# Block inverses of an RWKV-7 recurrence: alternating the two heads of a pair in the small matmuls that build them

## The chip, the cores and the metric

One core of a Trainium2 chip (trn2). The metric is device time in microseconds of one execution of the whole program, lower is better. TensorE is called PE below, its weight loads PEld, VectorE DVE, ScalarE ACT, GpSimd POOL; SP issues the DMAs.

## The reference, cut to what matters

The model is two layers on 512 tokens of 1024 features. Layer 0 mixes tokens by RWKV-7, layer 1 by a Conformer convolution; each is followed by cross-attention to 256 memory tokens and a conv-gated MLP. Only the recurrence of layer 0 is touched by the change:

```python
def rwkv7_step(S, inp):
    r_t, dec_t, k_t, v_t, kk_t, a_t = inp
    sa = jnp.einsum('bhij,bhj->bhi', S, -kk_t)
    S = (S * dec_t[:, :, None, :]
         + sa[..., None] * (kk_t * a_t)[:, :, None, :]
         + v_t[..., None] * k_t[:, :, None, :])
    y = jnp.einsum('bhij,bhj->bhi', S, r_t)
    return S, y
```

There are 16 heads of 64. The kernel does not step through 512 tokens. It cuts them into 8 chunks of 64; inside a chunk the terms `sa` depend on one another through a strictly lower triangular 64x64 matrix, so that each (head, chunk) needs the inverse of one unit triangular 64x64 matrix. That is 128 inverses. Each is built from two 32x32 inverses on the diagonal and a 32x32 block that couples them.

## The kernel before, in words

All weight products (`gemm_cols`, `mm3`, lines 179 to 223) split both operands into a high and a low fp32r part and make three matmuls of 128x128 weights on 512 columns (L181, L182, L183). The weights come by DMA, ACT rounds them to the high part (L176) and DVE subtracts (L177). Layer 0 runs the products for k, r and v one after another, eight output blocks each. After each block a callback does the pair's own work (`k_done`, `r_done`, `v_done`) and then `step(n)`, which at fixed places starts a stage of the inverses. A pair is two heads, head h on partitions 64h to 64h+63.

The 16 heads are two groups of four pairs. For each group there are two stages:

- `subst_a` (lines 563 to 602), after the blocks k 3 (group 0) and r 4 (group 1). **Set-up products**: for each of four pairs one PSUM tile ("kv", one bank); for head h, chunk c and half u one matmul of 64x32 weights (`bk`) on 64 or 32 columns (`AR`), L577. The output stands on partitions 64h+32u. DVE masks the diagonal blocks (L580), two ACT copies take the off-diagonal ones into `TT` (L584). Then DVE alone inverts all 32x32 diagonal blocks at once by forward substitution, 30 steps of a multiply (L598) and an add (L600), with 32x32 transposes before (L586).
- `subst_b` (lines 604 to 635), after the blocks r 1 (group 0) and v 5 (group 1). DVE transposes the inverses into `D1` (L608) and `DT` (L610). **Coupling products**: for head h and half of the 32 (pair, chunk) blocks, 16 matmuls of 32x32 weights on 32 columns into one kv bank (L622), one ACT copy of 32x512 into `RT` (L624); then, for head h and half again, 16 such matmuls (L632) and one ACT copy into `TT` (L634). With q1 = partitions 64h to 64h+31 and q2 = the next 32, L622 reads q1 and writes q2, L632 reads q2 and writes q1. `TT` also gets two ACT copies of `DT` per head (L616, L617) and a memset on POOL (L615).

The kv tag has two buffers (line 139), which also serve the products of keys and values of the memory (L912, L936). They stand between the others as fillers. Each engine works through a queue in order. That order is fixed when the kernel is built: the framework's scheduler takes the instructions in the order of the program, as priorities, moves ready ones ahead by its own estimates of their durations, and adds the semaphores.

After v comes `chain` (lines 637 to 759), the recurrence over the eight chunks, which multiplies by `TT` in L711; there the two heads of a pair already alternate in the innermost loop and write one bank.

A plain-fp32 matmul of the program stands in the trace as two matmul instructions, each with its own weight load: 256 matmuls of L577 are 512 rows, 128 of L622 and of L632 are 256 each.

Of the kernel before, what the change touches and what calls it, by code (L numbers as in the profile page):

```python
# [21 lines left out]
NCH = T // C  # L22
# [88 lines left out]
class Builder:  # L111
# [451 lines left out]
    def subst_a(self, grp):  # L563

        nc = self.nc
        TT = self.TT[grp]
        rho = self.rho[:, grp * 32 : grp * 32 + 32]
        c4 = lambda: self.t(self.r1, [128, 32, 32], "c4", bufs=4)
        A = c4()
        for pl in range(4):  # L570
            p = grp * 4 + pl
            ps = self.ps("kv").rearrange("p (c t) -> p c t", t=64)
            for h in range(2):
                rows = slice(64 * h, 64 * h + 64)
                for c in range(NCH):
                    for u in range(2):
                        nc.tensor.matmul(ps[64 * h + 32 * u : 64 * h + 32 * u + 32, c, 0 : 64 - 32 * u],  # L577
                                         self.bk[p][rows, c, h, 32 * u : 32 * u + 32],
                                         self.AR[rows, 0, p, c * C + 32 * u : (c + 1) * C], start=True, stop=True)
            nc.vector.tensor_tensor(out=A[:, pl * 8 : pl * 8 + 8, :], in0=ps[:, :, 0:32],  # L580
                                    in1=self.c("m32").unsqueeze(1).to_broadcast([128, 8, 32]), op=ALU.mult)
            for h in range(2):
                q1 = slice(64 * h, 64 * h + 32)
                nc.scalar.copy(TT[q1, pl * 8 : pl * 8 + 8, 32:64], ps[q1, :, 32:64])  # L584
        N = c4()
        nc.vector.transpose(out=N, in_=A.rearrange("p g t -> p t g"))  # L586
        rt = self.t(self.r1, [128, 32], "rt", bufs=1)
        nc.vector.transpose(out=rt, in_=rho)
        nc.vector.tensor_tensor(out=N, in0=N, in1=rt.unsqueeze(2).to_broadcast([128, 32, 32]), op=ALU.mult)
        Ti = c4()  # L590
        nc.scalar.copy(Ti, N)
        nc.vector.memset(Ti.rearrange("p t s -> p (t s)")[:, 0 : 32 * 32 : 33], 1.0)
        prs = c4().rearrange("p g t -> p (g t)")
        for s in range(1, 31):
            n = 31 - s
            pr = prs[:, s % 2 * 512 :]
            pv = pr[:, : n * s].rearrange("p (t j) -> p t j", j=s)
            nc.vector.tensor_tensor(out=pv, in0=N[:, s + 1 :, s : s + 1].to_broadcast([128, n, s]),  # L598
                                    in1=Ti[:, s : s + 1, 0:s].to_broadcast([128, n, s]), op=ALU.mult)
            nc.vector.tensor_tensor(out=Ti[:, s + 1 :, 0:s], in0=Ti[:, s + 1 :, 0:s], in1=pv, op=ALU.add)  # L600
        nc.vector.tensor_tensor(out=Ti, in0=Ti, in1=rt.unsqueeze(1).to_broadcast([128, 32, 32]), op=ALU.mult)
        self.sub = TT, Ti, c4

    def subst_b(self, grp):
        nc = self.nc
        TT, Ti, c4 = self.sub
        D1 = c4()
        nc.vector.transpose(out=D1.rearrange("p g j -> p j g"), in_=Ti.rearrange("p t j -> p j t"))  # L608
        DT = c4()
        nc.vector.transpose(out=DT.rearrange("p g t -> p t g"), in_=Ti)  # L610
        RT = c4().rearrange("p g t -> p (g t)")
        for h in range(2):
            q1 = slice(64 * h, 64 * h + 32)
            q2 = slice(64 * h + 32, 64 * h + 64)
            nc.gpsimd.memset(TT[q2, :, 0:32], 0.0)  # L615
            nc.scalar.copy(TT[q1, :, 0:32], DT[q1])  # L616
            nc.scalar.copy(TT[q2, :, 32:64], DT[q2])  # L617
            for half in range(2):
                ps = self.ps("kv")
                for j in range(16):  # L620
                    g = half * 16 + j
                    nc.tensor.matmul(ps[q2, j * 32 : (j + 1) * 32], TT[q1, g, 32:64], D1[q1, g, :],  # L622
                                     start=True, stop=True)
                nc.scalar.copy(RT[q2, half * 512 : half * 512 + 512], ps[q2, :])  # L624
        for h in range(2):
            q1 = slice(64 * h, 64 * h + 32)
            q2 = slice(64 * h + 32, 64 * h + 64)
            for half in range(2):
                ps = self.ps("kv")
                for j in range(16):  # L630
                    g = half * 16 + j
                    nc.tensor.matmul(ps[q1, j * 32 : (j + 1) * 32], RT[q2, g * 32 : (g + 1) * 32],  # L632
                                     DT[q2, g, :], start=True, stop=True)
                nc.scalar.copy(TT[q1, half * 16 : half * 16 + 16, 32:64],  # L634
                               ps[q1, :].rearrange("p (g t) -> p g t", t=32))

    def chain(self):

# [741 lines left out]
```

## Time and profile before

| what | value |
|---|---|
| median of 3 runs (lowest to highest) | 1705.75 us (1701.08 to 1711.86) |
| the profiled execution's own time | 1704.39 us |
| its span | 1702.6 us |
| PE busy | 1668.6 us (98%) |
| DVE busy, ACT busy | 1096.9 us (64%), 782.5 us (46%) |
| mean granted clock of TensorE | 0.99 |

The span runs from the first to the last instruction of the program; 1.8 us of the execution lie outside it. Busy PE is not PE at its peak: the rows of matmuls overlap. The stages of the inverses lie between 101 and 299 us of the span; `chain` follows from 309 us.

### The profile page before, as it was taken

The page shows a single profiled execution, that of the slowest core. Times are in us where ns is not written, and L with a number is a line of the kernel's source. Part 1 is how long each engine was busy: PE and PEld are TensorE (multiplying, and loading weights), DVE is VectorE, ACT ScalarE, POOL GpSimd, SP SyncE. Part 2 cuts the span into 40 slices and gives each one's busy share as a digit, 9 for nine tenths or more (in the row PEclk, how much of TensorE's full clock was granted, in tenths as well). Part 3 has the DMA queues.
Part 4 walks back from the last instruction along what each step waited for, and adds up shares of the span by engine and source line. Part 5 has one row for each costly group of instructions (what it writes and reads, how often), then busy time and mean ns, then how long its engine had stood idle before and what let it go on. Part 6 is the DMA issues. An engine that isn't in the chain of part 4 may idle for free. (4 is left out here: it accounts for less than half of the span.)

```text
span 1702.6 us, 23980 instructions
## 1 busy us (share of the span) xinstructions
PE 1668.6 (98%) x9662; PEld 1328.1 (78%) x9662; DVE 1096.9 (64%) x1777; ACT 782.5 (46%) x1216; POOL 73.2 (4%) x101
## 2 busy tenths in 40 slices
PE   7999989999999999999999999999999999999998
PEld 6585668888788888888888877767888888888887
DVE  4679975344676567777753358996666677777333
ACT  5865634445435335444432256665444444444222
POOL 0000000000000000000000014340000000000000
PEclk9999999999999999999999999999999999999999
DMA  6323312001533232333333332223412233333332
GB/s 230 122 85 108 107 56 75 27 14 33 158 120 113 63 124 88 100 99 97 92 98 92 105 118 62 62 88 99 137 63 74 89 99 100 98 91 93 101 91 84
DMA packets 55151, 159.77 MB, mean 94 GB/s; under 512 B 6144, under 2 KB 10368, under 8 KB 55040
## 3 DMA queue, kind: packets, MB, share of 16 engines
q1 hardware_dynamic: 55040, 158.24, 29.9%
q8 instruction: 76, 1.25, 0.3%
q14 instruction: 35, 0.29, 0.1%
HBM read 150.55 MB, written 7.67 MB: 93 GB/s over the span
## 5 line engine op out<-in xcount | busy, mean ns | idle before, releaser
L176 ACT CAST wh<-raw 128x1024 fp32r<-128x1024 f32 (+1 forms) x225 | 233.2, 1037 | 496.6 <-PE g L182 406.6
L182 PE MATMUL g<-xl,wh 128*128 128x512 f32 x1152 | 452.2, 393 | 4.2 <-DVE xl L177 3.6
L181 PE MATMUL g<-xh,wh 128*128 128x512 f32 x1152 | 454.0, 395 | 0.6 <-ACT xh L176 0.6
L183 PE MATMUL g<-xh,wl 128*128 128x512 f32 x1152 | 451.9, 392 | 1.6 <-DVE wl L177 1.6
L177 DVE TENSOR_TENSOR wl<-raw,wh 128x1024 fp32r<-128x1024 f32 (+1 forms) x225 | 272.2, 1210 | 159.0 <-ACT wh L176 158.5
L182 PEld LDWEIGHTS g<-xl,wh 128*128 128x128 f32 x1152 | 217.5, 189 | 54.0 <-DVE xl L177 6.6
L183 PEld LDWEIGHTS g<-xh,wl 128*128 128x128 f32 x1152 | 217.5, 189 | 49.3 <-DVE wl L177 2.3
L181 PEld LDWEIGHTS g<-xh,wh 128*128 128x128 f32 x1152 | 217.4, 189 | 48.8 <-ACT xh L176 1.7
L181 PE MATMUL g<-ah,wh 128*128 128x512 f32 (+1 forms) x374 | 140.9, 377 | 0.0
L182 PE MATMUL g<-al,wh 128*128 128x512 f32 (+1 forms) x374 | 140.8, 377 | 0.0
L183 PE MATMUL g<-ah,wl 128*128 128x512 f32 (+1 forms) x374 | 140.8, 377 | 0.0
L1050 DVE TENSOR_TENSOR z<-g,rs 128x512 f32<-128x512 f32 x88 | 60.4, 688 | 71.3 <-PE g L183 69.7
L182 PEld LDWEIGHTS g<-al,wh 128*128 128x128 f32 x374 | 70.4, 188 | 13.0
L183 PEld LDWEIGHTS g<-ah,wl 128*128 128x128 f32 x374 | 70.4, 188 | 12.9
L181 PEld LDWEIGHTS g<-ah,wh 128*128 128x128 f32 x374 | 70.4, 188 | 12.7
L1170 POOL TENSOR_TENSOR dg<-i,wsp 128x256 fp32r<-128x256 f32 x70 | 48.3, 723 | 668.2 <-DVE wsp L1124 584.1
L1192 DVE SCALAR_TENSOR_TENSOR h<-u,cdw,h 128x512 f32<-128x512 f32 x98 | 73.8, 753 | 2.4
L176 ACT CAST ah<-tmp 128x512 fp32r<-128x512 f32 x44 | 27.3, 621 | 100.9 <-DVE z L1049 95.8
L321 DVE TENSOR_TENSOR x<-x,g 128x512 f32<-128x512 f32 x39 | 26.8, 688 | 67.5 <-PE g L183 67.5
L1055 DVE SCALAR_TENSOR_TENSOR tmp<-z,fdw,tmp 128x512 f32<-128x512 f32 x88 | 66.0, 752 | 2.9
L1054 DVE SCALAR_TENSOR_TENSOR tmp<-z,fdw,tmp 128x512 f32<-128x512 f32 x88 | 65.5, 746 | 0.4 <-ACT tmp L1053 0.4
L1053 ACT ACTIVATE tmp<-z,fdw 128x512 f32<-128x512 f32 x88 | 63.3, 722 | 4.8 <-DVE z L1050 1.5
(331 smaller groups left out, 2458.3 us busy)
## 6 DMA issues: line engine op xcount, KB each, us to landing
raw<-wi SPq DMA_DIRECT2D x84, 512.0 KB, 3.5
raw<-wo SPq DMA_DIRECT2D x33, 512.0 KB, 3.5
raw<-wv SPq DMA_DIRECT2D x16, 512.0 KB, 3.6
raw<-cwi SPq DMA_DIRECT2D x14, 512.0 KB, 3.5
raw<-wq SPq DMA_DIRECT2D x12, 512.0 KB, 4.6
raw<-wxo SPq DMA_DIRECT2D x12, 512.0 KB, 3.6
raw<-wo SPq DMA_DIRECT2D x16, 384.0 KB, 3.1
raw<-wk SPq DMA_DIRECT2D x10, 512.0 KB, 3.5
```

The source lines that it names most:

```text
L176: self.nc.scalar.copy(h, src)
L177: self.nc.vector.tensor_tensor(out=l, in0=src, in1=h, op=ALU.subtract)
L181: mm(out, lh, rh, start=start, stop=False)
L182: mm(out, lh, rl, start=False, stop=False)
L183: mm(out, ll, rh, start=False, stop=stop)
L321: self.nc.vector.tensor_tensor(out=self.x[:, n, :], in0=self.x[:, n, :], in1=ps, op=ALU.add)
L1050: nc.vector.tensor_tensor(out=z[:, 2:], in0=ps, in1=rs(), op=ALU.mult)
L1053: nc.scalar.activation(y, z[:, 2:], AF.Copy, scale=cw(2))
L1054: nc.vector.scalar_tensor_tensor(out=y, in0=z[:, 1 : T + 1], scalar=cw(1), in1=y, op0=ALU.mult, op1=ALU.add)
L1055: nc.vector.scalar_tensor_tensor(out=y, in0=z[:, 0:T], scalar=cw(0), in1=y, op0=ALU.mult, op1=ALU.add)
L1170: nc.gpsimd.tensor_tensor(out=dg[:, h], in0=i2.unsqueeze(1).unsqueeze(1).to_broadcast([128, 2, 2, 64]), in1=wsp[:, :, i, h, 2 * g : 2 * g ...
L1192: nc.vector.scalar_tensor_tensor(out=ac, in0=u[:, jt : jt + T], scalar=cw(jt), in1=ac if n else ln["c"], op0=ALU.mult, op1=ALU.add if n el ...
```

## The change

In `subst_a` the loops over chunk and half go outside and the loop over the two heads innermost: the same matmuls, in another order. In `subst_b` the same is done in both coupling products, and the tile is taken per half rather than per head and half: one kv bank holds the results of both heads (on disjoint partitions), 32 matmuls rather than 16, and two ACT copies empty it. So a group takes four kv tiles in `subst_b` and not eight. The memset and the copies of `DT` of both heads come ahead of the products in program order. The number, shape and engine of all instructions stay.

```diff
-            for h in range(2):
-                rows = slice(64 * h, 64 * h + 64)
-                for c in range(NCH):
-                    for u in range(2):
+            for c in range(NCH):
+                for u in range(2):
+                    for h in range(2):
+                        rows = slice(64 * h, 64 * h + 64)
                         nc.tensor.matmul(ps[64 * h + 32 * u : 64 * h + 32 * u + 32, c, 0 : 64 - 32 * u],
...
+        q1 = [slice(64 * h, 64 * h + 32) for h in range(2)]
+        q2 = [slice(64 * h + 32, 64 * h + 64) for h in range(2)]
         for h in range(2):
-            q1 = slice(64 * h, 64 * h + 32)
-            q2 = slice(64 * h + 32, 64 * h + 64)
-            nc.gpsimd.memset(TT[q2, :, 0:32], 0.0)
-            nc.scalar.copy(TT[q1, :, 0:32], DT[q1])
-            nc.scalar.copy(TT[q2, :, 32:64], DT[q2])
-            for half in range(2):
-                ps = self.ps("kv")
-                for j in range(16):
-                    g = half * 16 + j
-                    nc.tensor.matmul(ps[q2, j * 32 : (j + 1) * 32], TT[q1, g, 32:64], D1[q1, g, :],
+            nc.gpsimd.memset(TT[q2[h], :, 0:32], 0.0)
+            nc.scalar.copy(TT[q1[h], :, 0:32], DT[q1[h]])
+            nc.scalar.copy(TT[q2[h], :, 32:64], DT[q2[h]])
+        for half in range(2):
+            ps = self.ps("kv")
+            for j in range(16):
+                g = half * 16 + j
+                for h in range(2):
+                    nc.tensor.matmul(ps[q2[h], j * 32 : (j + 1) * 32], TT[q1[h], g, 32:64], D1[q1[h], g, :],
                                      start=True, stop=True)
-                nc.scalar.copy(RT[q2, half * 512 : half * 512 + 512], ps[q2, :])
...
+            for h in range(2):
+                nc.scalar.copy(RT[q2[h], half * 512 : half * 512 + 512], ps[q2[h], :])
...
+                for h in range(2):
+                    nc.tensor.matmul(ps[q1[h], j * 32 : (j + 1) * 32], RT[q2[h], g * 32 : (g + 1) * 32],
+                                     DT[q2[h], g, :], start=True, stop=True)
+            for h in range(2):
+                nc.scalar.copy(TT[q1[h], half * 16 : half * 16 + 16, 32:64],
+                               ps[q1[h], :].rearrange("p (g t) -> p g t", t=32))
```

The removed loops of L632 and L634, left out here, are those of L622 and L624 with q1 and q2 exchanged.

## Rows read from the trace of the kernel before

**Rows 1.** Windows of 10 us: each engine's busy us and instructions, PEclk, DMA share, GB/s.

```profile
100.00:110.00 10.00, 10.00 (x158) 8.35 (x157) 8.08 (x18) 5.81 (x12) 0.32 (x1) 1.00 0.30 93
110.00:120.00 10.00, 9.86 (x102) 7.61 (x101) 7.66 (x18) 7.57 (x14) 0.00 (x0) 1.00 0.29 93
...
180.00:190.00 10.00, 9.44 (x42) 6.93 (x41) 9.77 (x24) 5.00 (x10) 1.32 (x2) 1.00 0.22 61
190.00:200.00 10.00, 8.31 (x108) 6.81 (x108) 9.85 (x15) 9.01 (x12) 0.57 (x1) 0.66 0.66 228
200.00:210.00 10.00, 10.00 (x166) 6.76 (x166) 6.72 (x11) 4.09 (x7) 0.00 (x0) 1.00 0.01 2
...
220.00:230.00 10.00, 9.99 (x197) 8.00 (x195) 6.34 (x8) 3.49 (x9) 0.00 (x0) 1.00 0.18 56
...
290.00:300.00 10.00, 10.00 (x154) 8.55 (x151) 0.00 (x0) 2.88 (x5) 0.00 (x0) 0.61 0.02 3
```

**Rows 2.** Waits from 95 to 310 us: total us, times, longest us.

```profile
PE g L182 <- DVE xl L177: 3.6, 3, 2.6
...
DVE c L580 <- PE kv L577: 4.1, 5, 1.2
```

**Rows 3.** Groups of instructions by line, 101 to 310 us: weight loads.

```profile
L577 PEld LDWEIGHTS kv<-AR,BK 64*32 64x32 f32 x512 | 12.7, 106 | 3.0 <-issue 2.6 <-ACT tt L584 0.3
...
L632 PEld LDWEIGHTS kv<-c,c 32*32 32x32 f32 x256 | 10.1, 123 | 2.5 <-issue 1.8 <-ACT tt L634 0.7
...
L622 PEld LDWEIGHTS kv<-c,tt 32*32 32x32 f32 x256 | 8.4, 108 | 2.6 <-DVE c L608 1.1 <-issue 0.6 <-ACT tt L617 0.6
```

**Rows 4.** Timeline, weight loads: start us, length us, line, shape, count.

```profile
101.74 1.62 PEld L577 LDWEIGHTS kv<-AR,BK 64*32 64x32 f32 x64 [0.36 <-issue]
...
190.11 3.01 PEld L622 LDWEIGHTS kv<-c,tt 32*32 32x32 f32 x96 [1.11 <-DVE c L608]
...
200.16 1.08 PEld L622 LDWEIGHTS kv<-c,tt 32*32 32x32 f32 x32 [0.59 <-ACT tt L617]
...
204.48 3.01 PEld L632 LDWEIGHTS kv<-c,c 32*32 32x32 f32 x96 [0.36 <-issue]
...
284.09 2.10 PEld L622 LDWEIGHTS kv<-c,tt 32*32 32x32 f32 x64 [0.35 <-PE g L182]
...
290.91 4.15 PEld L632 LDWEIGHTS kv<-c,c 32*32 32x32 f32 x96 [0.25 <-issue]
...
296.28 1.78 PEld L632 LDWEIGHTS kv<-c,c 32*32 32x32 f32 x32 [0.65 <-ACT tt L634]
...
317.14 0.55 PEld L711 LDWEIGHTS h<-tmp,tt 64*64 64x64 f32 x16
```

**Rows 5.** Windows of 0.2 us, L577 alone: PE and PEld busy and count, PEclk.

```profile
102.00:102.20 0.20, 0.20 (x15) 0.20 (x10) 1.00 1.08 410
102.40:102.60 0.20, 0.20 (x22) 0.20 (x18) 1.00 0.73 266
```

**Rows 6.** Timeline around `subst_b` of group 0: DVE, PE and ACT.

```profile
193.53 1.22 DVE L177 TENSOR_TENSOR wl<-raw,wh 128x1024 fp32r<-128x1024 f32 x1
...
194.81 0.80 PE L183 MATMUL g<-xh,wl 128*128 128x512 f32 x1 [1.57 <-DVE wl L177]
...
196.71 0.58 ACT L624 COPY c<-kv 32x512 f32<-32x512 f32 x1
...
201.39 0.58 ACT L624 COPY c<-kv 32x512 f32<-32x512 f32 x1 [0.64 <-PE kv L622]
```

**Rows 7.** Timeline, large matmuls after `subst_b` of group 1.

```profile
299.14 0.63 PE L181 MATMUL g<-xh,wh 128*128 128x512 f32 x1
299.57 0.63 PE L182 MATMUL g<-xl,wh 128*128 128x512 f32 x1
...
305.01 0.39 PE L182 MATMUL g<-xl,wh 128*128 128x512 f32 x1
305.24 0.39 PE L183 MATMUL g<-xh,wl 128*128 128x512 f32 x1
```

More of the change, by code (lines that the diff above doesn't have):

```diff
@@ L625, in subst_b @@
[L625 to L635, printed above, removed]
+            nc.gpsimd.memset(TT[q2[h], :, 0:32], 0.0)
@@ new lines, in subst_b @@
+        for half in range(2):
+            ps = self.ps("kv")
+            for j in range(16):
+                g = half * 16 + j
+                for h in range(2):
[4 more added lines that the diff above has]
+                               ps[q1[h], :].rearrange("p (g t) -> p g t", t=32))
```

## The prediction, made before the changed kernel was run

> **What bounds the kernel now.** I read four views in turn: windows of 10 us over the stretch where the inverses are built (who is full there), the waits of that stretch (who waits for whom), the groups by line (how many instructions the change touches), and the timeline close to each stage (their spacing). The windows show two regimes. At 100 to 120, 200 to 210, 220 to 230 and 290 to 300 us PE is full (9.86 to 10.00 of 10) and DVE has room; at 180 to 200 us DVE is full (9.77, 9.85) and PE is not [rows 1]. The waits agree: DVE waits 4.1 us for the set-up products, and PE waits 3.6 us for DVE's low halves [rows 2]. So a microsecond saved on PE is worth a microsecond in the first regime, as long as the work behind it moves up too, and nothing while DVE is full.
>
> The touched matmuls are 1024 instructions, 512 in L577 and 256 each in L622 and L632 [rows 3]. They are small, and what they cost is their spacing, not the length of a row (a load lasts 0.106 us, and many are under way at once). With the last load's length taken off [rows 4]:
> - L577: (1.62 - 0.11) / 63 = 24.0 ns from one to the next;
> - L622 and L632: (3.01 - 0.11) / 95 = 30.5 ns;
> - L711, where the heads alternate: (0.55 - 0.135) / 15 = 27.7 ns, with 64 weight columns and 64 moving columns (0.135 for its last load is an estimate; at 0.11 it would be 29.3).
>
> So the alternating L711 streams twice the columns of L622 in less time for each instruction. I read that as two heads under way at once: one tile of 64 columns would need about twice the 30.5 ns. L577 gives a second sign. Its two halves u already stand on different output columns, while the two heads follow each other; at the change from head 0 to head 1, half of the way through the block, 18 loads touch a window of 0.2 us where 10 touch one in the middle of a head [rows 5]. There the end of one head runs beside the start of the next.
>
> **The change part by part.** No instruction is added or taken away; the alternation is what can save.
>
> 1. L577, eight blocks of 64 rows. If both heads run side by side, a block falls from 64 x 24.0 ns = 1.54 us to 0.77. Bounds: 0 (the spacing is already under that of L711) and 0.77 us a block. I take the latter, the half, since where the heads meet the density nearly doubles [rows 5]. Group 0: 4 x 0.77 = 3.1 us. PE is full there, and DVE has 1.92 + 2.34 = 4.3 us of idle time at 100 to 120 us [rows 1], more than 3.1, so the substitution, which then fills DVE up to 200 us, can start earlier by as much. Group 1: 3.1 us, PE full (9.99), DVE at 6.34. Sum 6.2, bounds 0 and 6.2.
> 2. L622 of group 0, 128 rows. The first 96, 3.01 us from 190.11, stand in a wait for DVE: PE's next large matmul starts at 194.81 whatever they take, since DVE gets to its weights at 193.53 [rows 6]. Worth nothing. The last 32 (1.08 us from 200.16 [rows 4]) are on PE's path: half is 0.5 us; if they fit into that wait as well, 1.1. I take 0.5; at the other end 0.
> 3. L632 of group 0, 128 rows: 3.01 us for 96 and in proportion 1.0 for the rest, 4.0 us with PE full at 200 to 210 us. Halved: 2.0. Bounds 0 and 2.0.
> 4. L622 of group 1, 128 rows: 2.10 us for 64 [rows 4], so 4.2, with PE busy throughout. Halved: 2.1. Bounds 0 and 2.1.
> 5. L632 of group 1, 128 rows: 4.15 + 1.78 = 5.9 us [rows 4], since the granted clock fell on the way (0.61 over 290 to 300 us [rows 1]); at full clock they would take the 4.0 of group 0. Halved at the same clock: 3.0. Bounds 0 and, at full clock throughout, 5.9 - 2.0 = 3.9.
> 6. The large matmuls after it. At the low level of the clock (1.2 GHz) they start 0.43 us apart, at the high one (2.4 GHz) 0.23 [rows 7]. The clock fell after PE had done little but small matmuls, and came back, with large ones under way, between 300 and 305 us. From the end of the 96 at 295.1, less the 1.78 us of the last 32, that is 3.1 to 8.1 us of large ones, 7 to 19 of them, which cost 0.20 us each more than at full clock: 1.4 to 3.8 us, in the middle 2.6. A stretch of small ones half as long may or may not spare this. Bounds 0 and 3.8; I take 0, the row as it stands.
> 7. Waits. A product now waits for two ACT copies of 0.58 us, one for each head, before its bank and its half of `RT` are free, where it waited for one [rows 6]. PE has large matmuls to put between, as before. Behind such a wait stand the next weight products, and behind them DVE and ACT. I charge one copy, 0.6 us; bounds 0 and four copies, 2.3.
>
> Sum: 6.2 + 0.5 + 2.0 + 2.1 + 3.0 - 0.6 = 13.2 us. The profiled execution took 1704.4 (a span of 1702.6 and 1.8 around it), so 1691.2. It lies 1.4 us under the median of 1705.75; for a median of the changed kernel I say 1692. Past 309 us nothing is touched, and I assume that the recurrence and the layers behind it move up unchanged. 1% is 17 us, about what a measurement of this kernel can tell from no change; the forecast lies just inside it.
>
> **A rule that speaks against it.** The two heads of L711 read different row halves, write one bank, and still start 27.7 ns apart [rows 4]. The Trainium skill (TensorEngine Tiling (Array Packing), "Restrictions and Gotchas") says that different row tiles cannot access the same PSUM bank at once. By that rule items 1 to 5 would give nothing, by the row they give the sum above. The trace doesn't bear the rule out for heads that also write different partitions of the bank, as they do here.
>
> **Rivals.**
> - *The bank makes the heads take turns.* At 32x32, each alternated pair then takes its two spacings of 30.5 ns, L577 its 24.0, and only the charge for waits is left: 1704.4 + 0.6 = 1705.0. For it: no row before has two 32x32 tiles side by side. Against it: L711, and the dense window of L577, whose heads share a bank too. This is what the Trainium skill's rule above would make of it.
> - *A floor for each instruction.* L622 and L632 fall from 30.5 to L577's 24.0 and L577 stays. For it: 24.0 and 27.7 are close although the columns differ. Against it: the dense window of [rows 5]. Gain: on the three stages of items 3 to 5, 128 x 6.5 ns = 0.8 us each, 2.4, less 0.6: 1702.6. The Trainium skill (TensorE: Matmul & The Clock Gate, "Wait — 56ns, not 53.3ns?") states such a floor, about 25 ns from start to start; the mean of 24.0 lies a little under it.
> - *DVE keeps it.* DVE is full before 200 us and the order of its queue is fixed. If earlier set-up products don't let the substitution start earlier, because DVE's other work stands before it, items 1 and 2 are lost: 13.2 - 6.7 = 6.5 us, 1697.9. For it: 9.77 and 9.85 of 10. Against it: DVE's 4.3 idle us before, and its waits for just these products [rows 2].
> - *The clock holds.* With half the time in small matmuls the clock doesn't fall at group 1: items 5 and 6 give 3.9 + 2.6, which is 3.5 more than taken: 1687.7. For it: the price stands there, 5.9 us and the large ones behind. Against it: the small ones that are left still come in one run.
> - *PE stands behind ACT (slower).* In group 0 the copies L624 were late, at 196.71 and 201.39 us, as ACT was at 9.01 of 10 and works in order. If PE's fixed order puts a product that needs both heads' copies ahead of the weight products, PE stands still from about 192 to 202, 10 us, and then has 16 large matmuls at the low clock (3.2 us); in group 1 it waits for four copies (2.3). That is 15.5 against 13.2 + 0.6: 1706.1. It decides from about 14 us of standing still.
>
> **How the numbers follow.** Chances: forecast 0.42, clock holds 0.20, DVE keeps it 0.20, floor 0.07, bank 0.04, PE behind ACT 0.07. The forecast's own range is 1688 to 1695 (item 6 in part; item 7 at its end). The whole range, 1684 to 1704, reaches from the clock rival with item 6 at its end, all of item 2 and no charge for waits (1685.3), less the 1 us or so by which runs differ, to beyond the floor rival; it leaves out the bank and ACT rivals and what may lie outside all of these. Faster by over 1% (under 1688.7): two thirds of the clock rival and a seventh of the forecast, 0.19. Slower by over 1% (over 1722.8): only if PE stands far longer, 0.02. Within 1%: 0.79.
>
> **What would show it.** Right would be: L577 in blocks of 64 of about 0.9 us and not 1.62; L622 and L632 15 to 16 ns apart, 64 rows in about 1.1 us; the first substitution step earlier by 2 to 3 us and `chain` by 12 to 14; PE still waiting for DVE near 190 us. Wrong would be: spacings near 24 or 30 ns (floor, bank); halved spacings but a `chain` that starts no more than 7 us earlier (DVE); PE waiting for L624 or L634 (ACT); or a difference made after `chain` has begun, where I see none.

## The result, and the profile after

| | before | after |
|---|---|---|
| median of 4 runs each (lowest to highest) | 1707.88 us (1701.08 to 1711.86) | 1688.01 us (1686.79 to 1693.23) |
| the profiled execution's own time | 1704.39 us | 1689.21 us |
| its span | 1702.6 us | 1687.3 us |
| its mean granted clock | 0.990 | 0.992 |

The ratio of the medians is 0.9884, 95% interval 0.9853 to 0.9915. The kernel became 1.2% faster: inside the range given, 4 us under the forecast of 1692, and just past the 1% that the forecast had stopped short of (the interval reaches to 0.85%; the repeat, e10, lies past 1% with all of its interval). It is the time of the rival "the clock holds" (1687.7).

In the changed kernel the first coupling product is L623 (was L622), its copy L626, the last copy L635 and the first product of `chain` L663; L577 and L632 keep their numbers. The timeline of the weight loads gives the new spacing, to be set against [rows 4]:

```profile
100.51 0.92 PEld L577 LDWEIGHTS kv<-AR,BK 64*32 64x32 f32 x64 [0.35 <-issue]
...
188.03 2.10 PEld L623 LDWEIGHTS kv<-c,tt 32*32 32x32 f32 x128 [1.13 <-DVE c L608]
...
200.69 2.10 PEld L632 LDWEIGHTS kv<-c,c 32*32 32x32 f32 x128 [0.36 <-issue]
...
278.45 2.10 PEld L623 LDWEIGHTS kv<-c,tt 32*32 32x32 f32 x128 [0.35 <-PE g L182]
...
281.96 2.10 PEld L632 LDWEIGHTS kv<-c,c 32*32 32x32 f32 x128 [0.37 <-issue]
```

All four coupling products take 2.10 us for 128 rows, (2.10 - 0.11) / 127 = 15.7 ns from one to the next, where it was 30.5. L577 takes (0.92 - 0.11) / 63 = 12.9 ns, where it was 24.0. The groups by line, 100 to 295 us, say the same in sums. Beside [rows 3] the busy time fell and the count did not; a load lasts as long as before, but for L632 (123 to 108 ns), part of which had run at the low clock:

```profile
L577 PEld LDWEIGHTS kv<-AR,BK 64*32 64x32 f32 x512 | 7.6, 106 | 4.2 <-issue 3.3 <-ACT tt L584 0.9
L632 PEld LDWEIGHTS kv<-c,c 32*32 32x32 f32 x256 | 4.2, 108 | 0.7 <-issue 0.7
L623 PEld LDWEIGHTS kv<-c,tt 32*32 32x32 f32 x256 | 4.2, 108 | 1.5 <-DVE c L608 1.1 <-PE g L182 0.4
```

The windows of 10 us (columns as in [rows 1]):

```profile
100.00:110.00 10.00, 9.51 (x159) 7.05 (x157) 7.02 (x17) 6.35 (x11) 0.32 (x1) 1.00 0.33 104
...
180.00:190.00 10.00, 9.30 (x153) 7.01 (x153) 9.77 (x20) 4.17 (x7) 1.89 (x2) 1.00 0.33 85
190.00:200.00 10.00, 7.53 (x36) 5.05 (x30) 9.76 (x16) 9.07 (x12) 0.00 (x0) 0.66 0.52 172
...
240.00:250.00 10.00, 7.14 (x20) 4.23 (x19) 9.88 (x21) 3.82 (x7) 0.00 (x0) 0.74 0.17 59
...
280.00:290.00 10.00, 10.00 (x202) 8.42 (x196) 0.64 (x1) 5.08 (x9) 0.00 (x0) 1.00 0.32 101
290.00:300.00 10.00, 9.88 (x105) 8.31 (x103) 2.58 (x4) 3.47 (x8) 0.00 (x0) 1.00 0.25 92
```

Three things are to be seen. PE is still idle for 2.5 us of 190 to 200 while DVE is full, as said. At 240 to 250 us PE waits for DVE too (7.14), and the clock fell there (0.74). In the trace of before PE is idle in the same way at 250 to 260 us, and the clock stayed at 1.00:

```profile
250.00:260.00 10.00, 6.51 (x25) 4.42 (x26) 9.94 (x21) 5.73 (x9) 0.00 (x0) 1.00 0.22 64
```

And at group 1 the granted clock now stays at 1.00 through both products and what follows, where it had fallen to 0.61. The large matmuls behind L632 show it, 0.24 us apart and not 0.43 [rows 7]:

```profile
284.44 0.40 PE L181 MATMUL g<-xh,wh 128*128 128x512 f32 x1
284.68 0.40 PE L182 MATMUL g<-xl,wh 128*128 128x512 f32 x1
```

**Where the time came from.** Landmarks of the two traces, us from the span's start:

| landmark | before | after | earlier by |
|---|---|---|---|
| first set-up block | 101.74 | 100.51 | 1.2 |
| first substitution step, group 0 | 138.88 | 136.78 | 2.1 |
| first set-up block of group 1 | 217.96 | 212.03 | 5.9 |
| first substitution step, group 1 | 230.54 | 224.07 | 6.5 |
| transposes into `D1`, group 1 | 272.95 | 267.30 | 5.7 |
| first product of `chain` | 308.96 | 294.07 | 14.9 |
| last output of `chain` | 435.84 | 419.48 | 16.4 |
| end | 1702.62 | 1687.35 | 15.3 |

The largest step, 9.2 us, lies between the transposes of group 1 and `chain`. The 1.2 us at the top came before anything that the change touches: the traced run of before had 3.4 us at the low clock from 29.4 us on, that of after none there.

**A line through all the runs.** Every run comes with its mean granted clock c. The low level is half of full speed, so the time that a run spent there is about 2 (1 - c) of its time. Later jobs brought 42 runs of before, with a median of 1711.5 us, from 1699.96 us (c = 0.992) to 1715.13 us (0.983). A straight line through them has a slope of 0.41 us for each microsecond at the low level and meets zero such time at 1690.1 us. With the same slope for all kernels the residual is 0.9 us (117 runs). I call that intercept the time at full clock; for each kernel it is the mean over its runs. By the scatter of those runs it is uncertain by 0.1 us (before) to 0.9 us (e5). It splits each difference below into "work", the difference at full clock, and clock. The split rests on the line; no run was held at one clock level.

### The profile page after: what moved, and what is told of

The parts are those of the page before. It is cut to its first block, busy times and chain, and to the rows that moved or that the text cites. A ratio compares the mean times of both kernels' runs of the same rounds, so it can differ in the third digit from the quotient of the medians.

```text
span 1687.3 us, 23987 instructions
## 1 busy us (share of the span) xinstructions
PE 1650.6 (98%) x9662; PEld 1312.3 (78%) x9662; DVE 1096.3 (65%) x1777; ACT 782.2 (46%) x1216; POOL 73.1 (4%) x101
## 5 line engine op out<-in xcount | busy, mean ns | idle before, releaser
L182 PEld LDWEIGHTS g<-al,wh 128*128 128x128 f32 x374 | 70.4, 188 | 12.9
L183 PEld LDWEIGHTS g<-ah,wl 128*128 128x128 f32 x374 | 70.4, 188 | 12.9
```

The costliest lines, as they stand in the source:

```text
L182: mm(out, lh, rl, start=False, stop=False)
L183: mm(out, ll, rh, start=False, stop=stop)
```

## The experiments

Each job ran the kernel before on the same chip. "Low" is the median time at the low level.

| kernel | median us (runs) | ratio to before, 95% | low us | at full clock |
|---|---|---|---|---|
| before | 1711.5 (42) | | 51.3 | 1690.1 |
| after, first comparison | 1688.0 (4) | 0.9884 (0.9853 to 0.9915) | 25.3 | 1677.9 |
| after, again (e10) | 1687.5 (4) | 0.9865 (0.9839 to 0.9891) | 21.9 | 1678.9 |
| e1 set-up only | 1704.0 (11) | 0.9962 (0.9946 to 0.9979) | 44.3 | 1686.2 |
| e2 coupling only | 1686.8 (5) | 0.9870 (0.9841 to 0.9898) | 13.5 | 1680.6 |
| e3 one bank, heads in turn | 1697.5 (10) | 0.9931 (0.9910 to 0.9951) | 25.5 | 1686.4 |
| e4 alternating, two banks | 1700.5 (11) | 0.9942 (0.9923 to 0.9961) | 34.0 | 1686.1 |
| e5 group 1 only | 1694.5 (4) | 0.9903 (0.9875 to 0.9932) | 25.4 | 1684.0 |
| e6 group 0 only | 1697.6 (5) | 0.9928 (0.9904 to 0.9952) | 27.2 | 1686.1 |
| e7 group 1 twice | 1700.7 (5) | 0.9936 (0.9915 to 0.9957) | 37.4 | 1684.3 |
| e8 wait filled | 1686.1 (4) | 0.9856 (0.9837 to 0.9875) | 18.5 | 1678.7 |
| e9 one copy | 1688.1 (4) | 0.9862 (0.9843 to 0.9880) | 23.6 | 1678.0 |
| e11 e8 and e9 | 1688.6 (4) | 0.9861 (0.9840 to 0.9883) | 20.3 | 1680.1 |
| e12 e8, set-up as before | 1689.3 (4) | 0.9866 (0.9847 to 0.9885) | 18.6 | 1681.6 |

**The two parts apart.** e1 is the kernel before with the first part of the change's diff alone, the new loop order of L577; e2 has the other part alone, the new `subst_b`.

> Only the set-up products (L577) alternate; the coupling products stay as before. My theory: a block of 64 falls from 1.62 us to 0.92, but little of it arrives, since the block's neighbours (the ACT copies that free its bank, the r and k callbacks that PE waits for) set the pace: 1 to 2 us faster, spacing of the coupling products still 31 ns, and the clock falls at group 1 as before. Rival 'every PE microsecond counts': 8 x 0.7 = 5.6 us faster. Rival 'clock': the shift alone moves where the clock falls, which gives anything within 4 us either way.

The blocks of L577 fall to 0.92 us. Eight of them save 5.6 us. But e1's trace, which leads that of before by 1.4 us at the first block (100.39 against 101.74), leads by 3.6 at the first product of `chain` (305.38 against 308.96): 2.2 arrive, 0.8 gained up to the first substitution step of group 0 and 1.2 over the set-up of group 1. The waits of e1 while group 1 is set up, 217 to 229 us, show who takes the rest:

```profile
DVE c L580 <- PE kv L577: 1.6, 2, 1.1
...
PEld h L553 <- DVE tmp L550: 0.9, 1, 0.9
...
PEld kv L577 <- ACT tt L584: 0.6, 1, 0.6
```

In the trace of before DVE waits there for L577 for 2.9 us, PE for L550 for 0.2 and for L584 not at all. So PE got ahead of the work between the blocks and then stood. At full clock the part is worth 3.9 us. In the median it is 7.1 us (the 26 runs of before on that chip had 1711.06), since e1 also spent less time at the low level: outside all three expectations.

> Only the coupling products alternate, both heads in one bank; the set-up products stay as before. My theory: the coupling products carry the gain, by halved spacing (16 ns) and by the clock that no longer falls at group 1: 12 to 15 us faster, the recurrence starts at about 296 us and not 309. Rival 'halved rows alone': the products give 2 + 2 + 3 us and the clock still falls: 7 to 8 us faster, the recurrence starts at about 301 us.

e2 carries the gain: both halves of each product in one run of 128 rows of 2.10 us, `chain` from 295.15 us, 24 us less in the median, where 12 to 15 were expected. In work that is 9.5 us, above the 7.6 of items 2 to 5; the rest is clock (51.3 to 13.5 us low). In work e1 and e2 together make 13.4 us, the whole change 11.6 (both comparisons of it). In the median e2 alone is as fast as the whole change (1686.8 against 1688.0 and 1687.5): on top of e2 the set-up's alternation shows no gain there, only in the time at full clock.

**Pairing, or the shared bank?** e3 keeps the one bank for two heads but runs the heads one after the other; e4 alternates them but gives each its bank. Both have the set-up of before.

```diff
-            for j in range(16):
-                g = half * 16 + j
-                for h in range(2):
+            for h in range(2):
+                for j in range(16):
+                    g = half * 16 + j
```

The second product is edited in the same way.

> As the run with the coupling products alone, one bank for both heads, half the tiles and the same order of the copies, but inside a bank all 16 of head 0 come ahead of head 1. My theory: no pairing, so 31 ns from one to the next, the small matmuls of group 1 last 8 us and the clock falls there: within 3 us of the kernel before. Rival 'fewer banks to wait for': the gain is in the arrangement, 8 us or more faster although the spacing stays at 31 ns.

```profile
188.02 4.20 PEld L623 LDWEIGHTS kv<-c,tt 32*32 32x32 f32 x128 [1.12 <-DVE c L608]
...
289.47 6.34 PEld L632 LDWEIGHTS kv<-c,c 32*32 32x32 f32 x128 [0.65 <-issue]
```

In this timeline of e3 the spacing is that of before, (4.20 - 0.11) / 127 = 32 ns, and at group 1 the clock falls again, so that the same 128 rows take 6.34 us. Its windows there:

```profile
280.00:290.00 10.00, 10.00 (x158) 8.17 (x157) 2.45 (x2) 5.79 (x9) 0.00 (x0) 0.84 0.37 112
290.00:300.00 10.00, 10.00 (x132) 9.07 (x131) 0.00 (x0) 2.30 (x4) 0.00 (x0) 0.50 0.01 3
```

So the halved spacing does need the alternation. `chain` starts only 1.0 us earlier than before, in a trace that led by 2.1 us at the first set-up block. But the median fell by 13.6 us: far outside the 3 us expected, and by the number it is the rival's 8 us or more. By the line 3.7 us of that is work, the rest less time at the low level, which one trace does not place. The whole first product of group 0 now stands in one row ahead of the wait for DVE; that this and the fewer banks to empty make the 3.7 us is not shown.

```diff
-            ps = self.ps("kv")
+            pss = [self.ps("kv") for _ in range(2)]
...
-                    nc.tensor.matmul(ps[q2[h], j * 32 : (j + 1) * 32], TT[q1[h], g, 32:64], D1[q1[h], g, :],
+                    nc.tensor.matmul(pss[h][q2[h], j * 32 : (j + 1) * 32], TT[q1[h], g, 32:64], D1[q1[h], g, :],
```

The copies read `pss[h]`, and the second product is edited in the same way.

> As the run with the coupling products alone, alternating, but each head writes a bank of its own, so a half takes both kv banks. My theory: the heads run side by side in one bank as well as in two, so the spacing is 16 ns in both, and the next half waits for two banks to be emptied, with 0.6 to 1.2 us of copies four times: 0 to 4 us slower than one bank. Rival 'the bank holds the heads up': with two banks the spacing falls well under 16 ns and the time is shorter than with one bank.

The timeline of e4's weight loads at group 1:

```profile
285.75 1.09 PEld L623 LDWEIGHTS kv<-c,tt 32*32 32x32 f32 x64 [0.35 <-PE g L182]
...
288.47 1.08 PEld L623 LDWEIGHTS kv<-c,tt 32*32 32x32 f32 x32 [0.36 <-ACT c L626]
289.59 0.19 PEld L181 LDWEIGHTS g<-xh,wh 128*128 128x128 f32 x1
290.01 1.08 PEld L623 LDWEIGHTS kv<-c,tt 32*32 32x32 f32 x32 [0.24 <-issue]
```

With a bank for each head 64 alternating rows take 1.09 us, 15.6 ns: as in one bank. So sharing the bank costs no spacing. What two banks cost is order: the second half of this product waits for a copy, its heads fall apart, and each stands alone at 31 ns. e4 is 5.5 us slower than e2 at full clock and spent 20 us more at the low level. Pairing and sharing belong together here: one of them alone (e3, e4) gives 4 us of work, both give 9.5.

**Which group, and what of it is the clock?** e5 uses the new `subst_b` for group 1 only, e6 for group 0 only, with the set-up of before; the old one is kept as `subst_b_seq`, and `subst_b_alt` is that of the change. e5's line is shown; e6 has `grp == 0`.

```diff
+        (self.subst_b_alt if grp == 1 else self.subst_b_seq)(grp)
```

> The coupling products alternate in group 1 alone; group 0 and the set-up products stay as before. My theory (rows and clock): the 128 rows of each product of group 1 fall from 4.2 and 5.9 us to 2.1 and 2.1, the clock stays at its high level there, and from the end of the substitution to the start of the recurrence 8 to 9.5 us are gained; in the median 9 to 15 us, since runs in which the clock falls for longer than in the profiled one gain more. Rival 'rows alone': the clock still falls at group 1 and 5 us are gained there, 5 to 7 in the median.

From the transposes of group 1 to `chain` e5 takes 26.88 us, before 36.01, after 26.77: 9.1 us as expected, and its clock is 1.00 from 280 to 300 us. In the median it gained 15.6 us, just over the 9 to 15 expected. The windows of e5 show that the clock fell at group 0 instead, over 200 to 220 us, where the second product is still done head by head (1.00 over 200 to 210 us in after, but also in before, which has the same order there):

```profile
200.00:210.00 10.00, 10.00 (x130) 5.98 (x129) 6.18 (x10) 2.78 (x5) 0.00 (x0) 0.76 0.02 3
210.00:220.00 10.00, 10.00 (x39) 5.61 (x39) 1.62 (x3) 0.58 (x1) 0.00 (x0) 0.73 0.16 53
```

> The coupling products alternate in group 0 alone; group 1 and the set-up products stay as before. My theory: the first product stands under PE's wait for DVE and gains nothing, its last 32 rows and the second product give about 3 us, and the clock falls at group 1 as before: 2 to 5 us faster in the median. With the run on group 1 alone the two gains add up to that of both groups (about 1.3%). Rival 'the low clock of group 0 is half the story': 8 us or more, with several us less at the low level around 190 to 210 us.

Expected were 2 to 5 us, measured 12.5: missed, and by the number it is the rival, 8 us or more. In work the part is worth 4.0 us; the rest is time at the low level (51.3 to 27.2). One trace each doesn't place it: over 190 to 200 us e6 has 0.83 where before has 0.66, 3.4 us less at the low level. e6's trace has the clock at 1.00 over 200 to 210 us, and falls at group 1, like before:

```profile
280.00:290.00 10.00, 10.00 (x205) 8.79 (x203) 1.11 (x1) 3.98 (x8) 0.00 (x0) 0.87 0.30 100
290.00:300.00 10.00, 10.00 (x56) 7.78 (x56) 0.00 (x0) 1.56 (x3) 0.00 (x0) 0.62 0.08 20
```

The two groups don't add up: 15.6 and 12.5 us alone, 24 together in e2. In work they do as far as can be told, 6.1 + 4.0 = 10.1 against 9.5. A lesson in reading: what is not additive here is the clock, not the work.

e7 asks whether the clock holds because the small matmuls are denser or because they are over sooner. It runs each alternating product of group 1 twice (the second time over the same results), so the density was to be that of after and the length that of before. Both products have this edit.

```diff
-            for j in range(16):
+            for j in list(range(16)) * (1 + grp):
```

> As the changed kernel, but in group 1 each coupling matmul is issued twice (the same result is written again), so the small products last as long as they did before the change, 4.2 us each, while the two heads still run side by side. Theory 'density': it is the pairing that holds the clock, so it stays high, and the cost over the changed kernel is the rows, 4.2 us: about 1692. Rival 'brevity': the clock held because the stretch of small products was short; twice as long it falls again, and 4.2 us of rows, slower rows and some 13 large matmuls at 0.43 us make it 8 to 10 us slower than the changed kernel: 1696 to 1698.

The windows of e7 at group 1:

```profile
270.00:280.00 10.00, 10.00 (x164) 8.36 (x164) 4.38 (x4) 7.25 (x8) 0.00 (x0) 1.00 0.33 90
280.00:290.00 10.00, 8.34 (x328) 8.14 (x322) 0.14 (x1) 3.46 (x6) 0.00 (x0) 0.59 0.22 73
290.00:300.00 10.00, 10.00 (x104) 8.44 (x101) 0.00 (x0) 1.74 (x3) 0.00 (x0) 0.73 0.01 3
...
280.80:281.60 0.80, 0.00 (x0) 0.00 (x0) 0.00 (x0) 0.58 (x1) 0.00 (x0) 1.00 0.57 146
281.80:282.20 0.40, 0.00 (x0) 0.00 (x0) 0.00 (x0) 0.00 (x0) 0.00 (x0) 0.50 0.73 256
```

The median of 1700.7 us lies above both expectations (1692; 1696 to 1698), and at full clock e7 is 5.8 us slower than the change. But it doesn't decide the question. The clock fell at 281.8 us, and the last two windows show PE without a single instruction there: behind 2.6 us of small matmuls it stood still for 1.7 us, and the clock fell 1.1 us into that. It stayed down for 13.7 us. So the standstill is a rival to the length, and neither is shown to be the cause. Over all traces the clock held at group 1 in all eight in which both products were paired in one bank and issued once (after, e2, e5, e8 to e12), and fell in the six others (before, e1, e3, e4, e6, e7). That is a pattern and not a cause. Length alone doesn't explain it: in e4 the clock fell at 291.5 us behind rows of 1.1 us with large matmuls between them, while in after it held through two rows of 2.1 us. What holds the clock stays open.

**What is left.** In group 0 the clock still falls in after, at 190.3 us for 6.8 us. The first product has then just ended, and PE's wait for DVE only begins:

```profile
188.00:190.20 2.20, 2.17 (x128) 2.10 (x128) 2.20 (x2) 1.31 (x3) 0.46 (x1) 1.00 0.73 260
190.20:190.60 0.40, 0.04 (x4) 0.00 (x0) 0.40 (x1) 0.40 (x1) 0.00 (x0) 0.59 1.04 399
```

e8 puts three plain matmuls of 128x512 ahead of the first product's second half there, into the same bank, which the product then overwrites.

```diff
             ps = self.ps("kv")
+            for _ in range(3 if grp == 0 and half else 0):
+                nc.tensor.matmul(ps, self.c("ident"), D1.rearrange("p g j -> p (g j)")[:, 0:512], start=True, stop=True)
```

> As the changed kernel, with three plain-fp32 matmuls of 128 columns on 512 (0.86 us each) put between the halves of the first product of group 0, where PE otherwise waits 2.5 us for DVE; their results are overwritten. Theory: they fill a wait and cost nothing, and the clock, which falls at 190 us with PE waiting, falls there less often or for less time: 0 to 3 us faster than the changed kernel. Rival 'the wait has no part in it': the clock falls as before, 0 to 1 us slower.

```profile
190.00:200.00 10.00, 10.00 (x216) 6.93 (x215) 9.79 (x16) 9.24 (x13) 0.00 (x0) 1.00 0.45 138
```

In this window of e8 PE is full and the clock 1.00, where it was 7.53 and 0.66. The clock also holds there in e11 and e12, and falls within 190 to 200 us in all traces without the three matmuls. They fill the wait, but they also part the halves of the small product; which of the two counts is not tested. The median of 1686.1 us lies 1.4 to 1.9 under that of after, but the intervals of the ratios overlap: not shown to be faster.

e9 removes the second ACT copy behind L577, which PE waited for in e1. The matmuls of u = 1 write their 32 columns twice, so that one copy over both heads and both halves can fill `TT` (the lines that set `ar` and `out`, and the matmul itself, are left out):

```diff
+                        if u:
+                            ar = ar.unsqueeze(1).to_broadcast([64, 2, 32])
+                            out = out.rearrange("p (a t) -> p a t", a=2)
...
-            for h in range(2):
-                q1 = slice(64 * h, 64 * h + 32)
-                nc.scalar.copy(TT[q1, pl * 8 : pl * 8 + 8, 32:64], ps[q1, :, 32:64])
+            nc.scalar.copy(TT[:, pl * 8 : pl * 8 + 8, 32:64], ps[:, :, 32:64])
```

> As the changed kernel, but a block of set-up products is emptied by one ACT copy of all 128 partitions where there were two of 32 (0.36 us each); for that the matmuls of the second half stream their 32 columns twice, and the rows of TT that get the surplus are overwritten later, as before. Theory 'emptying and feeding': of the 5.6 us that the set-up blocks are shorter, some is lost because a block waits for its bank (0.6 us before the last block of group 1) and the rest to the callbacks of k and r, which this leaves: the wait for the copy goes, the substitution of group 1 starts 0.3 to 0.8 us earlier after its first block, and the time stays within 2 us of the changed kernel. Rival 'the banks are all of it': 2 us earlier or more.

From the first set-up block of group 1 to the first substitution step it takes 10.99 us where after takes 12.04 (and e10, the same kernel as after, 12.59), but the time is unchanged (1688.1).

Three kernels ran beside e9: e10 is the changed kernel once more, e11 joins e8 and e9, e12 is e8 with the set-up loops of before.

> The changed kernel itself, on the same chip as the three beside it: 1686 to 1692, with the low clock of its runs at 20 to 37 us. If it is the clock that spreads the runs, each us at the low level costs about 0.41 us here too.

> The changed kernel with both: the filled wait of group 0 and the one copy for a block. Expected 0 to 3 us faster than the changed kernel and within 1 us of the filled wait alone; the low clock of its runs at 17 to 20 us. Rival: the two shift the stages against each other and the clock falls elsewhere, no faster than the changed kernel.

> Coupling products alternating and the wait filled, the set-up products as before the change. What the set-up's alternation is worth when the clock is out of it: theory 2 to 4 us slower than the filled wait with it (about 1688 to 1690), since only part of the 5.6 us arrives. Rival 'nothing arrives': the same time as with it.

e10 gives 1687.5 us and so confirms the first comparison. e11 is no better than either part, 2.5 us above e8 where 1 was expected. e12 against e8, at the same time at the low level (18.6 and 18.5 us), puts the set-up's alternation at 3.2 us in the medians and 2.9 at full clock; they ran on different chips, and the intervals of their ratios overlap. No version is shown to beat the changed kernel.

## Why the prediction was right, and where it was off

- **The mechanism** was right. Two heads run side by side: 15.7 ns (15 to 16 said), L577 in blocks of 0.92 us (0.9 said). The rivals "the bank makes the heads take turns" and "a floor for each instruction" fell with those rows. The Trainium skill (TensorEngine Tiling (Array Packing), "Restrictions and Gotchas") says that different row tiles cannot access one bank at the same time; here 15.7 ns in one bank and 15.6 in two (e4) show no such cost, so the measurement decides. The Trainium skill (TensorE: Matmul & The Clock Gate, "Wait — 56ns, not 53.3ns?") has about 25 ns as the least from start to start; here it is 12.9 and 15.7 ns between instructions on different tiles, and again the measurement decides.
- **Item 1 (set-up, 6.2 us taken, bounds 0 to 6.2)** was mis-sized. The blocks saved 5.6 us, but 2.1 (after against e2), 2.9 (e12 against e8) or 3.9 (e1) arrived at full clock. The first substitution step came 2.1 us earlier, of which 1.2 was there before the change begins; 2 to 3 was said. The failed step is the clause "the substitution ... can start earlier by as much": it took DVE's 4.3 idle us as room. Of the 4.1 us for which DVE waited for these products only 1.2 fall in group 0, and most of DVE's idle time there was spent waiting for ACT. Its waits in the trace of before, 100 to 140 us:

```profile
DVE tmp L531 <- ACT tmp L525: 3.2, 2, 1.9
DVE G L521 <- ACT AR L518: 1.4, 2, 0.7
DVE c L580 <- PE kv L577: 1.2, 2, 1.1
```

  In e1 the last of these is 0.5, so 0.7 us less, close to the 0.8 that arrived there; the first two are 3.5 and 1.4. In group 1 PE was full only until the blocks were fast enough for L553 to wait for DVE and L577 for the copies. That is the rival "DVE keeps it" in part.
- **Item 2 (0.5)**: the first part stood in the wait for DVE, as said (PE's next large matmul at 192.72 still waits 2.5 us), and the last 32 fitted into that wait as well: the upper end, 1.1.
- **Items 3 and 4 (2.0, 2.1)**: both products went from 4.0 and 4.2 us to 2.10. Right.
- **Item 5 (3.0)**: 5.9 us became 2.10, so 3.8, close to the upper end of 3.9, since the clock held.
- **Item 6 (0 taken, bounds 0 to 3.8)** failed: "I take 0, the row as it stands". Between the end of the last small matmuls and `chain` nothing ran at the low level. In the trace of before some 12 large ones did, from 295.1 us on, and 0.20 us for each of them makes 2.4 us (an estimate). Items 4 to 6 with the taken numbers make 5.1 us, the upper ends of 5 and 6 with item 4 make 9.8; measured were 9.2 (e5: 9.1).
- **Item 7 (-0.6)** was not paid, and its sign seems to be wrong: e3, which shares the bank without pairing the heads, is 3.7 us faster than before at full clock. (The 5.5 us of e2 against e4 are no clean price of it, since e4 also lost the pairing in half of the first product.) This partly stands against the shortfall of item 1.
- **PE behind ACT** did not come: PE's order puts large matmuls first, and no wait for L626 or L635 is among those of PE.
- **The step from one execution to the median.** Trace against trace the difference was 15.2 us, 2.0 more than the 13.2 of the sum. The forecast then assumed that the profiled run stood for the kernel ("it lies 1.4 us under the median"). It was one of the good ones: c = 0.990, some 34 us at the low level, against 51 in the median of 42 runs. From before to after (8 runs of it, low 23.6 us) the medians differ by 24 us; the line places 11.6 of it as work (1690.1 - 1678.5) and (51.3 - 23.6) x 0.41 = 11.4 as clock. The work is about the sum made for full clock, 13.2 less the 1.0 by which item 5 counted the low clock, 12.2. By this split, what put the result past 1% was the clock, in and beyond the stage that the change touches; the prediction gave 0.79 to a change within 1% and 0.19 to one beyond. That the median lies within 0.3 us of the rival "the clock holds" is partly luck: the rival left out the other stretches at the low level and took the whole of item 1. Which of those stretches (374 and 408 us in the trace of before, 245 and 392 in that of after) come and go with the change, and why, stays open: there is one trace for each kernel, and they differ there even between kernels that are alike (e10, the same kernel as after, has 141 and 325 us besides).

## What to carry to other kernels

The small matmuls here (64x32 and 32x32 weights) cost their spacing, and that spacing about halved when neighbours in the queue used other rows and other output partitions. Let such neighbours share a bank, so that one wait and one round of copies serve all of them. Count what a faster stage gives only up to the next engine that the stages between it wait for. And compare kernels with the granted clock of each run beside its time: a change may be worth as much by the time at the low level that goes with it as by the work that it saves, and a trace or two do not say why.

## What the runs showed of the hardware that was not expected

- L577, whose neighbours now go through four tiles in turn (two heads, two halves u), starts an instruction each 12.9 ns, where it took 24.0 with two tiles in turn. Two 32x32 tiles in turn take 15.7 ns.
- A microsecond at the low level costs 0.41 us of this kernel's time, and this accounts for nearly all of the 15 us over which the runs of before spread (1699.96 to 1715.13).
- The clock fell beside a wait of PE of 2.5 us (0.66 over 190 to 200 us in after), and not when three matmuls filled it (1.00 in e8, e11 and e12). The wait alone doesn't do it: in after the clock fell as the wait began, and in the trace of before PE was idle for 3.5 us of 250 to 260, at 1.00.
- The same kernel differs in this from run to run (c of after from 0.989 to 0.995).
